# Five raw buffers of streamed fp32 blocks as one tile with strictly rotating slots, in a single-core DiT block

## The chip, the cores and the metric

The kernel runs on one core of one Trainium2 chip. The metric is the device time of one execution in microseconds. A NeuronCore has TensorE (PE, with its weight loads shown apart as PEld), VectorE (DVE), ScalarE (ACT), GpSimd (POOL) and SyncE (SP). SP here does little else than issue DMAs, one after the other, from one instruction queue.

## What is computed

One layer of a diffusion transformer on 256 latent and 256 context tokens, width 2048, all in fp32, followed by a final norm. The reference, cut down:

```python
mod = (silu(c) @ w_ada + b_ada)[:, None, :]
sh1, sc1, g1, sh2, sc2, g2 = split(mod, 6)
h = modulate(rmsnorm(x, norm1_g), sh1, sc1)           # context tokens likewise
dq, dk, dv, mq, mk, mv, ga, gb = project(h, w_in, w_uq, w_ukv)
o_da  = diff_attend(dq, dk_all, dv_all, lam)          # 8 heads, two softmax maps each
o_mla = softmax_attend(mq, mk_all, mv_all, MLA_SCALE) # 8 heads, low-rank q and kv
x = x + g1 * ((sigmoid(ga) * (o_da @ w_o_da) + sigmoid(gb) * (o_mla @ w_o_mla)) @ w_out)
x = x + g2 * ((silu(h2 @ w_gate) * (h2 @ w_up)) @ w_down)
return rmsnorm(x, final_norm_g)
```

Two streams of HBM data matter here: the weights of the big projections, and `w_ada`, of which the kernel needs a matrix-vector product (a gemv) for each modulation vector.

## The kernel before, in words

**Weights.** Every projection is a sum over k of weight blocks of 128 x 1024 fp32 values (512 KB). `load_w` (line 159) takes a buffer tagged `raw` from the pool `stream`, which has five of them, and issues one DMA on SP (line 161). `split_w` (line 164) divides the block into a high part `wh`, cast by ACT (line 169), and a low part `wl`, which DVE gets by subtracting `wh` from `raw` (line 170). TensorE then multiplies three products, wh by the activations' high and low parts and wl by the high part, in `GroupT` and `group_b` (matmuls at lines 155 and 157). `wh` and `wl` have three buffers each. One block, called a unit below, feeds 24 matmuls: 16 with wh and 8 with wl. The last reader of a raw buffer is the subtraction on DVE.

**Gemv blocks.** `gemv` (line 495) streams `w_ada` in blocks of the same shape through the same five `raw` buffers (DMA at line 503) and accumulates on DVE: `gacc = raw * c + gacc` (line 507, and line 505 for the first of 16). One gemv block has one reader only, this DVE operation, whose output every next one needs. The gemv is a Python generator that runs in the background. A stage calls `tick` (line 371), and each tick writes the next block's DMA and accumulation into the program. Through attention and through the gate, output and merge projections (`ga`, `gb`, `yab`, lines 835 to 852, and `wo`, lines 874 to 893), three chunks of `w_ada` are worked off in this way. In the `ga`, `gb` and `yab` stages `every(2)` (line 376) gives one gemv block per two weight units. In the FFN, from the third of eleven column groups on, `gate.rest(tick)` (line 949) gives one gemv block per gate unit, for chunk 5.

**Order.** The Tile scheduler sets the order of the instructions on each engine, not the source alone. It works with the buffers' releases: a tile of the tag `raw` gets the buffer that comes free first, so which buffer a load takes is decided while scheduling. Each load's DMA waits for the DVE operation that last read its buffer, and SP issues the loads in its fixed order.

**The lead.** For a DMA into a raw buffer, count on DVE the operations that read raw blocks (lines 170, 505 and 507) from the one that releases the buffer to the one that reads the new block. That count is called the lead of the load below. A load with lead 3 is issued when the third raw-reading operation before its own reader has ended.

**Attention.** For the four pairs of heads `p` of the differential attention the program puts the projections of the next pair, gemv blocks and the softmax on the same engines. On DVE the splits `dvl` (line 548) and the maximum (line 641) stand in order with wl and gacc. ACT's exponential (line 642) waits for the maximum, and the scores' matmuls (`ps`, line 676) wait for ACT to have read the bank.

Of the kernel before, what the change touches and what calls it, by code (L numbers as in the profile page):

```python
# [11 lines left out]
F32 = mybir.dt.float32  # L12
# [6 lines left out]
P = 128  # L19
# [77 lines left out]
def kernel(  # L97
# [9 lines left out]
    def pool(name, bufs=1, space=None, side=None):  # L107
        st = ExitStack()
        kw = {}
        if space is not None:  # L110
            kw["space"] = space
        if side is not None:
            kw["side"] = side
        pl = st.enter_context(tc.tile_pool(name=name, bufs=bufs, reuse_waits="tile", **kw))
        return pl, st.close
# [3 lines left out]
    stream, _c1 = pool("stream")  # L119
# [19 lines left out]
    def nm(s):  # L139
        uid[0] += 1  # L140
        return f"{s}{uid[0]}"


    class Acc:
# [6 lines left out]
        def mm(self, region, lhsT, rhs, last=False):  # L151
# [4 lines left out]
            else:  # L156
                nc.tensor.matmul(region, lhsT, rhs, start=False, stop=last, skip_group_check=key != self.lead)  # L157

    def load_w(src, a, n):
        raw = stream.tile([P, 1024], F32, tag="raw", name=nm("raw"), bufs=5)  # L160
        nc.sync.dma_start(out=raw[:, : a * n], in_=src)
        return raw[:, : a * n].rearrange("p (a n) -> p a n", a=a)

# [9 lines left out]
    def wunit(w, k0, a, c0, n):  # L173
        return split_w(load_w(w.block(k0, a, c0, n), a, n), a, n)
# [257 lines left out]
    def first_group(k0, nk):  # L432

        v = load_w(w_in.block(k0, nk, 3584, 320), nk, 320)
        wh = stream.tile([P, 1024], F32R, tag="wh", name=nm("wh"), bufs=3)
        wl = stream.tile([P, 1024], F32R, tag="wl", name=nm("wl"), bufs=3)
# [4 lines left out]
        nc.scalar.copy(h1[:, :, 320:], h1[:, :, 256:320].bitcast(F32))  # L441
        nc.scalar.copy(l1[:, :, 320:], l1[:, :, 256:320].bitcast(F32))
        h2, l2 = split_w(load_w(w_in.block(k0, nk, 1024, 512), nk, 512), nk, 512)

        def cut(i, n):
# [49 lines left out]
    def gemv(chunk, sink):  # L495


        for hf in range(2):
            a = const.tile([P, 1024], F32, tag="gacc", name=nm("gacc"), bufs=1)
            c0 = chunk * D + hf * 1024  # L500
            for kt in range(KT):
                raw = stream.tile([P, 1024], F32, tag="raw", name=nm("raw"), bufs=5)
                nc.sync.dma_start(out=raw, in_=w_ada[kt * P : (kt + 1) * P, c0 : c0 + 1024])
                if kt == 0:
                    nc.vector.tensor_scalar_mul(a, raw, cols[:, kt : kt + 1])
                else:
                    nc.vector.scalar_tensor_tensor(a, raw, cols[:, kt : kt + 1], a, op0=ALU.mult, op1=ALU.add)  # L507
                if kt < KT - 1:
                    yield
            yield from sink(hf, a)  # L510
# [158 lines left out]
    def da_attention(h, q, k, v):  # L669
# [23 lines left out]
        split(oTa[0][:, h, :], oTa[1][:, h, :], y)  # L693

    bg[0] = chain(gemv(2, to_cols(g1c, 2)), gemv(4, to_cols(sc2c, 4)), gemv(3, to_cols(sh2c, 3)))
    for p in range(4):
        if p == 0:
# [230 lines left out]
    def keep(hf, a):  # L928
# [7 lines left out]
        yield  # L936

    bg[0] = gemv(5, keep)

    for g in range(11):  # L940
# [96 lines left out]
```

## Time and profile before

| what | us |
|---|---|
| runs of the kernel | 1600.13, 1592.73, 1602.61 |
| their median | 1600.13 |
| the profiled execution | 1590.97 |
| its span, first to last instruction | 1589.2 |

The profile shows the one profiled execution. Times in rows are microseconds from the span's start. A row of the timeline has start, busy time, engine, line, operation, tiles, and in brackets how long the engine was idle before it and what ended that. "x2" in such a row means two operations drawn together. `SPq` and the like are an engine's instruction queue, where DMAs are issued. Matmul ends are modelled, so a busy TensorE says that it had work, not that it ran at its peak.

### The profile page before, as it was taken

The page shows a single profiled execution, that of the slowest core. Times are in us where ns is not written, and L with a number is a line of the kernel's source. Part 1 is how long each engine was busy: PE and PEld are TensorE (multiplying, and loading weights), DVE is VectorE, ACT ScalarE, POOL GpSimd, SP SyncE. Part 2 cuts the span into 40 slices and gives each one's busy share as a digit, 9 for nine tenths or more (in the row PEclk, how much of TensorE's full clock was granted, in tenths as well). Part 3 has the DMA queues.
Part 4 walks back from the last instruction along what each step waited for, and adds up shares of the span by engine and source line. Part 5 has one row for each costly group of instructions (what it writes and reads, how often), then busy time and mean ns, then how long its engine had stood idle before and what let it go on. Part 6 is the DMA issues. An engine that isn't in the chain of part 4 may idle for free.

```text
span 1589.2 us, 28863 instructions
## 1 busy us (share of the span) xinstructions
PE 1536.9 (97%) x11966; PEld 1443.3 (91%) x11966; DVE 1015.8 (64%) x1360; ACT 736.8 (46%) x1038; POOL 16.1 (1%) x14
## 2 busy tenths in 40 slices
PE   3899999998999999999999999999999999999997
PEld 2678899998899999999999999999999999888886
DVE  5437887787896667677777566767555545455454
ACT  4335455545675444444446444444444444344343
POOL 0000000000000000000000000000000000011010
PEclk9999999999999999999999999999999999999999
DMA  9894653456454787878884668888566656665563
GB/s 369 338 366 161 210 176 111 139 176 202 150 160 162 258 280 259 291 266 296 299 280 148 229 226 300 289 271 280 196 191 196 197 192 220 194 192 197 191 193 120
DMA packets 100595, 356.34 MB, mean 224 GB/s; under 512 B 10993, under 2 KB 13553, under 8 KB 100209
## 3 DMA queue, kind: packets, MB, share of 16 engines
q1 hardware_dynamic: 99600, 351.58, 65.9%
q10 hardware_dynamic: 864, 2.93, 0.5%
q8 instruction: 93, 1.52, 0.4%
q14 instruction: 38, 0.30, 0.1%
HBM read 352.37 MB, written 2.10 MB: 223 GB/s over the span
## 4 chain that ended last, share of the span: by engine, by line
PE 72%; DMA 9%; DVE 6%; issue 1%; ACT 1%; DVEq 0%; POOLq 0%; POOL 0%; ACTq 0%
PE gate L157 15%; PE up L157 15%; PE down L157 15%; DMA raw<-in_w_ada_dram 9%; PE ga L157 4%; PE dv L157 4%; PE gb L157 3%; DVE gacc L507 3%; PE dk L157 2%; DVE wl L170 2%; PE yab L157 2%; PE wo L157 2%; PE dq L157 1%; PE cq L157 1%; PE pt L647 1%
## 5 line engine op out<-in xcount | busy, mean ns | idle before, releaser
L170 DVE TENSOR_TENSOR wl<-raw,wh 128x1024 fp32r<-128x1024 f32 (+1 forms) x453 | 548.9, 1222 | 326.9 <-ACT wh L169 312.6
L169 ACT CAST wh<-raw 128x1024 fp32r<-128x1024 f32 (+1 forms) x453 | 474.9, 1051 | 572.7 <-PE down L157 134.9
L507 DVE SCALAR_TENSOR_TENSOR gacc<-raw,cols,gacc 128x1024 f32<-128x1024 f32 x120 | 154.0, 1283 | 123.5 <-DMA raw<-in_w_ada_dram 123.2
L157 PE MATMUL gate<-h,wh 128*128 128x256 f32 x1386 | 175.9, 277 | 0.0
L157 PE MATMUL up<-h,wh 128*128 128x256 f32 x1386 | 175.8, 277 | 0.0
L157 PE MATMUL down<-wh,hid 128*128 128x512 f32 x696 | 173.3, 389 | 0.0
L157 PEld LDWEIGHTS up<-h,wh 128*128 128x128 f32 x1386 | 166.4, 188 | 0.1
L157 PEld LDWEIGHTS gate<-h,wh 128*128 128x128 f32 x1386 | 166.5, 188 | 0.0
L157 PEld LDWEIGHTS down<-wh,hid 128*128 128x128 f32 x696 | 130.7, 188 | 27.0
L157 PE MATMUL gate<-h,wl 128*128 128x256 f32 x704 | 96.7, 277 | 0.0
L157 PE MATMUL up<-h,wl 128*128 128x256 f32 x704 | 96.7, 277 | 0.0
L157 PE MATMUL down<-wl,hid 128*128 128x512 f32 x352 | 94.6, 389 | 0.0
L157 PEld LDWEIGHTS up<-h,wl 128*128 128x128 f32 x704 | 87.8, 188 | 0.2 <-DVE wl L170 0.2
L157 PEld LDWEIGHTS gate<-h,wl 128*128 128x128 f32 x704 | 87.8, 188 | 0.1
L157 PEld LDWEIGHTS down<-wl,hid 128*128 128x128 f32 x352 | 66.1, 188 | 13.7
L157 PE MATMUL ga<-hl,wh 128*128 128x256 f32 x504 | 65.6, 278 | 0.0
L157 PE MATMUL wo<-mT,wh 128*128 128x256 f32 x504 | 64.2, 278 | 0.0
L157 PE MATMUL gb<-hl,wh 128*128 128x256 f32 x504 | 64.0, 278 | 0.0
L157 PEld LDWEIGHTS ga<-hl,wh 128*128 128x128 f32 x504 | 61.4, 188 | 0.6 <-ACT wh L169 0.4
L157 PEld LDWEIGHTS wo<-mT,wh 128*128 128x128 f32 x504 | 60.6, 188 | 0.4 <-issue 0.4
L157 PEld LDWEIGHTS gb<-hl,wh 128*128 128x128 f32 x504 | 60.7, 188 | 0.0
L408 PE MATMUL pgb<-sraw,c 128*32 128x512 f32 (+1 forms) x288 | 32.8, 597 | 17.4 <-DMA sraw<-in_w_mod_dram 17.4
(334 smaller groups left out, 2316.5 us busy)
## 6 DMA issues: line engine op xcount, KB each, us to landing
raw<-in_w_ada_dram SPq DMA_DIRECT2D x128, 512.0 KB, 4.2
raw<-in_w_in_dram SPq DMA_DIRECT2D x119, 512.0 KB, 4.6
raw<-in_w_ffn_gate_dram SPq DMA_DIRECT2D x88, 512.0 KB, 4.4
raw<-in_w_ffn_up_dram SPq DMA_DIRECT2D x88, 512.0 KB, 4.4
raw<-in_w_ffn_down_dram SPq DMA_DIRECT2D x88, 512.0 KB, 3.6
sraw<-in_w_mod_dram SPq DMA_DIRECT2D x64, 512.0 KB, 8.5
raw<-in_w_out_dram SPq DMA_DIRECT2D x32, 512.0 KB, 5.1
raw<-in_w_o_da_dram SPq DMA_DIRECT2D x16, 512.0 KB, 4.8
```

The costliest lines, as they stand in the source:

```text
L157: nc.tensor.matmul(region, lhsT, rhs, start=False, stop=last, skip_group_check=key != self.lead)
L169: nc.scalar.copy(h, v)
L170: nc.vector.tensor_sub(l, v, h.bitcast(F32))
L408: nc.tensor.matmul(pgb[32 * j : 32 * j + 32, :w], c32[:, kt, :], vs[kt], start=kt < 4, stop=kt >= 12, tile_position=(0, 32 * j))
L507: nc.vector.scalar_tensor_tensor(a, raw, cols[:, kt : kt + 1], a, op0=ALU.mult, op1=ALU.add)
L647: nc.tensor.transpose(pt[:, j * P : (j + 1) * P], a[:, j * P : (j + 1) * P], ident)
```

## The change

The five `raw` buffers are no longer five tiles of a pool. They are one tile `raws` of 128 x 5 x 1024 values, allocated once, and a function hands out its five slots strictly in turn, in the order in which the loads are written in the program. Both users, `load_w` and `gemv`, call it. The memory is the same size, the number and shape of DMAs, casts, subtractions, accumulations and matmuls is the same.

```diff
+    raws = stream.tile([P, 5, 1024], F32, name="raws")
+    loads = [0]
+
+    def raw_tile():
+
+        loads[0] += 1
+        return raws[:, loads[0] % 5, :]
+
     def load_w(src, a, n):
-        raw = stream.tile([P, 1024], F32, tag="raw", name=nm("raw"), bufs=5)
+        raw = raw_tile()
         nc.sync.dma_start(out=raw[:, : a * n], in_=src)
...
             for kt in range(KT):
-                raw = stream.tile([P, 1024], F32, tag="raw", name=nm("raw"), bufs=5)
+                raw = raw_tile()
                 nc.sync.dma_start(out=raw, in_=w_ada[kt * P : (kt + 1) * P, c0 : c0 + 1024])
```

All later lines move down by eight: line 161 of before is 169 of after, 170 is 178, 503 is 511, 507 is 515, 548 is 556, 641 is 649. The order of SP's 681 DMAs differs at 228 places, all in the stretches where gemv blocks run beside weights. In the FFN's column groups 6 to 10 and in the down projection the order is the same as before.

The DMA issues on SP in the second of the four `ga`/`gb`/`yab` groups, four gemv blocks (`in_w_ada`) and the eight weight units of `w_o_da` and `w_o_mla` that they alternate with. Before:

```order
241 L503 DMA raw_7009<-in_w_ada_dram 128x1024
242 L161 DMA raw_7017<-in_w_o_da_dram 128x1024
243 L161 DMA raw_7047<-in_w_o_da_dram 128x1024
244 L503 DMA raw_7077<-in_w_ada_dram 128x1024
245 L161 DMA raw_7080<-in_w_o_da_dram 128x1024
246 L161 DMA raw_7110<-in_w_o_da_dram 128x1024
247 L503 DMA raw_7140<-in_w_ada_dram 128x1024
248 L161 DMA raw_7147<-in_w_o_mla_dram 128x1024
249 L161 DMA raw_7177<-in_w_o_mla_dram 128x1024
250 L503 DMA raw_7207<-in_w_ada_dram 128x1024
251 L161 DMA raw_7210<-in_w_o_mla_dram 128x1024
252 L161 DMA raw_7240<-in_w_o_mla_dram 128x1024
```

The same twelve loads after the change:

```order
188 L511 DMA raws<-in_w_ada_dram 128x1024
189 L169 DMA raws<-in_w_o_da_dram 128x1024 x3
190 L511 DMA raws<-in_w_ada_dram 128x1024
191 L169 DMA raws<-in_w_o_da_dram 128x1024
192 L169 DMA raws<-in_w_o_mla_dram 128x1024
193 L511 DMA raws<-in_w_ada_dram 128x1024
194 L169 DMA raws<-in_w_o_mla_dram 128x1024 x2
195 L511 DMA raws<-in_w_ada_dram 128x1024
196 L169 DMA raws<-in_w_o_mla_dram 128x1024
```

Before, a gemv load stands first of its three and takes the slot that its own predecessor's accumulation leaves. After, a weight load stands in that place. The gemv load stands one or two places later and takes the slot that a weight's subtraction leaves.

Counted over both programs, the leads of the 128 gemv loads are:

| lead | 1 | 2 | 3 | 4 | 5 | 6 and more |
|---|---|---|---|---|---|---|
| gemv loads before | 4 | 17 | 64 | 25 | 14 | 4 |
| gemv loads after | 1 | 37 | 33 | 32 | 16 | 9 |

In the first of the four `ga`/`gb`/`yab` groups four gemv loads lose one lead and one gains two, in the second (561 to 632 us of the trace) six lose one and two gain one, in the third four lose one and three gain one. In `wo` one loses and one gains. In each of the four FFN groups with gemv two lose one, and two later ones gain one.

The DVE instructions ahead of the softmax of the fourth pair in attention, from the gemv accumulations to the first maxima (`c<-ps`). Before:

```order
460 L507 SCALAR_TENSOR_TENSOR gacc_3632<-raw_4455,cols,gacc_3632 128x1024
461 L507 SCALAR_TENSOR_TENSOR gacc_3632<-raw_4488,cols,gacc_3632 128x1024
462 L170 TENSOR_TENSOR wl_4395<-raw_4392,wh_4394 128x1024
463 L507 SCALAR_TENSOR_TENSOR gacc_3632<-raw_4521,cols,gacc_3632 128x1024
464 L170 TENSOR_TENSOR wl_4428<-raw_4425,wh_4427 128x1024
465 L548 TENSOR_TENSOR dvl_4170<-dv_3939,dvh_4169 128x256
466 L548 TENSOR_TENSOR dvl_4170<-dv_3940,dvh_4169 128x256
467 L641 TENSOR_REDUCE c_4188<-ps_4184 128x1
```

The same place after the change:

```order
458 L515 SCALAR_TENSOR_TENSOR gacc_3569<-raws,cols,gacc_3569 128x1024 x2
459 L178 TENSOR_TENSOR wl_4312<-raws,wh_4311 128x1024
460 L515 SCALAR_TENSOR_TENSOR gacc_3569<-raws,cols,gacc_3569 128x1024
461 L556 TENSOR_TENSOR dvl_4090<-dv_3867,dvh_4089 128x256
462 L556 TENSOR_TENSOR dvl_4090<-dv_3868,dvh_4089 128x256
463 L649 TENSOR_REDUCE c_4108<-ps_4104 128x1
```

The subtraction `wl` that stood directly ahead of `dvl` (row 464 of before) stands behind the maxima in the changed program.

## Rows read from the trace of the kernel before

**Rows 1.** The page's first lines: span, busy time of each engine, share, instructions.
```profile
span 1589.2 us, 28863 instructions
...
PE 1536.9 (97%) x11966; PEld 1443.3 (91%) x11966; DVE 1015.8 (64%) x1360; ACT 736.8 (46%) x1038; POOL 16.1 (1%) x14
```

**Rows 2.** Busy time by stretch; columns: stretch, length, PE, PEld, DVE, ACT, POOL, clock, DMA share, GB/s.
```profile
0.00:40.00 40.00, 15.65 (x101) 8.89 (x102) 22.04 (x45) 17.09 (x27) 0.73 (x5) 0.91 0.97 369
600.00:640.00 40.00, 38.53 (x335) 37.59 (x334) 29.64 (x29) 15.94 (x17) 0.00 (x0) 1.00 0.81 266
1100.00:1140.00 40.00, 40.00 (x351) 39.82 (x351) 22.31 (x22) 18.07 (x19) 0.00 (x0) 1.00 0.64 209
```

**Rows 3.** The page's costliest groups, DVE; busy, mean ns of one, idle before, releaser.
```profile
L170 DVE TENSOR_TENSOR wl<-raw,wh 128x1024 fp32r<-128x1024 f32 (+1 forms) x453 | 548.9, 1222 | 326.9 <-ACT wh L169 312.6
...
L507 DVE SCALAR_TENSOR_TENSOR gacc<-raw,cols,gacc 128x1024 f32<-128x1024 f32 x120 | 154.0, 1283 | 123.5 <-DMA raw<-in_w_ada_dram 123.2
```

**Rows 4.** Timeline of DVE, second ga/gb/yab group, then third.
```profile
601.20 1.28 DVE L507 SCALAR_TENSOR_TENSOR gacc<-raw,cols,gacc 128x1024 f32<-128x1024 f32 x1 [2.59 <-DMA raw<-in_w_ada_dram]
602.40 2.36 DVE L170 TENSOR_TENSOR wl<-raw,wh 128x1024 fp32r<-128x1024 f32 x2
606.20 1.28 DVE L507 SCALAR_TENSOR_TENSOR gacc<-raw,cols,gacc 128x1024 f32<-128x1024 f32 x1 [1.43 <-DMA raw<-in_w_ada_dram]
...
624.02 1.28 DVE L507 SCALAR_TENSOR_TENSOR gacc<-raw,cols,gacc 128x1024 f32<-128x1024 f32 x1 [2.98 <-DMA raw<-in_w_ada_dram]
...
716.93 2.35 DVE L170 TENSOR_TENSOR wl<-raw,wh 128x1024 fp32r<-128x1024 f32 x2
```

**Rows 5.** Timeline of SP's DMA issues in the same group.
```profile
602.51 0.33 SPq L503 DMA_DIRECT2D raw<-in_w_ada_dram  x1
603.65 1.47 SPq L161 DMA_DIRECT2D raw<-in_w_o_mla_dram  x2
```

**Rows 6.** Timeline of PE, first matmuls with a wl, second and third group.
```profile
628.90 1.21 PE L157 MATMUL ga<-hl,wl 128*128 128x256 f32 x8 [1.36 <-DVE wl L170]
...
696.20 1.20 PE L157 MATMUL ga<-hl,wl 128*128 128x256 f32 x8 [0.37 <-DVE wl L170]
...
718.20 1.20 PE L157 MATMUL gb<-hl,wl 128*128 128x256 f32 x8
```

**Rows 7.** The gemv loads at line 503: time from issue to landing.
```profile
DMA to landing us min/median/max: 3.3/4.2/6.4
```

**Rows 8.** Timeline of DVE, end of the FFN's gate groups 2 to 5.
```profile
961.42 2.38 DVE L170 TENSOR_TENSOR wl<-raw,wh 128x1024 fp32r<-128x1024 f32 x2
...
1004.85 1.22 DVE L170 TENSOR_TENSOR wl<-raw,wh 128x1024 fp32r<-128x1024 f32 x1
...
1049.52 2.41 DVE L170 TENSOR_TENSOR wl<-raw,wh 128x1024 fp32r<-128x1024 f32 x2
...
1095.66 1.22 DVE L170 TENSOR_TENSOR wl<-raw,wh 128x1024 fp32r<-128x1024 f32 x1
```

**Rows 9.** Timeline of PE, the matmuls that use those wl.
```profile
963.35 0.62 PE L157 MATMUL gate<-h,wl 128*128 128x256 f32 x4
...
1006.87 0.62 PE L157 MATMUL gate<-h,wl 128*128 128x256 f32 x4
...
1052.94 0.64 PE L157 MATMUL gate<-h,wl 128*128 128x256 f32 x4
...
1098.16 0.64 PE L157 MATMUL gate<-h,wl 128*128 128x256 f32 x4
```

**Rows 10.** Timeline of DVE ahead of the fourth pair's softmax.
```profile
368.55 1.28 DVE L507 SCALAR_TENSOR_TENSOR gacc<-raw,cols,gacc 128x1024 f32<-128x1024 f32 x1 [2.43 <-DMA raw<-in_w_ada_dram]
369.75 1.22 DVE L170 TENSOR_TENSOR wl<-raw,wh 128x1024 fp32r<-128x1024 f32 x1
370.89 0.75 DVE L548 TENSOR_TENSOR dvl<-dv,dvh 128x256 fp32r<-128x256 f32 x2
```

**Rows 11.** Timeline of PE at that softmax.
```profile
373.10 0.80 PE L676 MATMUL ps<-dk,dq 128*128 128x512 f32 x1 [5.96 <-ACT t L642]
```

## The prediction

> **What bounds the kernel now.** I read the page first. TensorE is busy 1536.9 of 1589.2 us, 97%, and DVE 64% [rows 1], so the kernel is bound by TensorE nearly everywhere. The table of stretches says where it is not. In the first 40 us TensorE works 15.65 us, with the DMA engines at 0.97: that is the start, where weights come in, and the change doesn't reorder it. From 600 to 640 us it works 38.53 of 40, and in the FFN without gemv 40.00 of 40 [rows 2]. The reader is to see from this that there is little to win. TensorE is idle for 1589.2 - 1536.9 = 52.3 us [rows 1], of which 40 - 15.65 = 24.4 lie in the first 40 us [rows 2]. The other 28 us, 1.8%, are all there is, and the largest gap among them that the change touches is the 5.96 us of [rows 11]. What the change can do more easily is to lengthen waits.
>
> The costliest DVE groups say which waits there are. The accumulation gacc costs 1283 ns and was idle for 123.5 us in 120 runs, nearly all for its own block's DMA. The subtraction wl costs 1222 ns [rows 3]. DVE works in order, so while gacc waits for a gemv block the wl behind it waits too, and wl is what TensorE needs. In the second ga/gb/yab group a round of one gemv block and two weight units goes like this: gacc starts at 601.20 after a wait of 2.59 us, the two wl take 2.36, the next gacc waits 1.43 and starts at 606.20 [rows 4]. SP issues the gemv load at 602.51, when gacc at 601.20 has ended, and the two weight loads at 603.65 and after [rows 5]. So the gemv load goes out as soon as its predecessor is accumulated and uses the two wl as cover (lead 3). TensorE at first doesn't feel it, since wl run ahead of it. But such rounds take a little longer than TensorE's two units, the advance is used up, and at 628.90 TensorE waits 1.36 us for wl, in the next group 0.37 at 696.20 [rows 6]. At 718.20 [rows 6] it uses a wl that ended at about 718.15, the first of the two in the row at 716.93 [rows 4]. DVE sets the pace at these points, and what comes on top of its rounds there is paid in full.
>
> **What the change does to this, part by part.** The instructions are the same in number and shape, so nothing is added or removed on any engine, and the slots are the same 512 KB. What changes is the slot that a load takes. Before, a load takes the first free buffer. A gemv load gets the one that its own predecessor leaves, as gaccs run ahead of the wl of weights written earlier in the program. After, it takes the slot of the load five before it in the written order, which mostly is a weight's. That slot is free one DVE operation later. The order pieces show it: weight loads move ahead, the gemv load one or two places back.
>
> *The price of one lost lead.* The load is issued 603.65 - 602.51 = 1.14 us later [rows 5], by one wl. Whether the wait of gacc grows by 1.14 depends on how long the load takes. The trace shows 3.3 us at least, 4.2 in the median and 6.4 at most [rows 7]. If the later load, with fewer loads behind it, took 3.3 where it took 4.2, the price is 1.14 - 0.9 = 0.2 us. If it took 6.4, because a weight load is now in flight ahead of it, it is 1.14 + 2.2 = 3.3 us. I take 1.2, near the 1.14 of the issue with an unchanged median, as the gemv load has one weight load about 1.1 us from it in either order: before it stood behind, now it stands ahead. A gained lead gives back the same, if gacc waited there.
>
> *Second group.* Six gemv loads lose a lead. Two gain one: the first at 624.02, where gacc waited 2.98 us [rows 4] and gives 1.2 back, the second behind the point that counts. At 628.90 TensorE already waits, so the sum is paid there: (6 - 1) x 1.2 = 6.0 us.
>
> *Third group.* Two losses and a gain stand ahead of 696.20, where TensorE waits 0.37 us: 1.2 us. Behind it a gain and two losses come before 718.20, where wl is just in time: 1.2 us. Together 2.4. The last gain of this group lies where nothing waits. The first group loses four and gains two, but the timeline of TensorE shows no gap there that ends on a wl, so I take nothing. In wo one loss and one gain cancel.
>
> *FFN groups with gemv.* Each has two losses and, for certain, one gain: 1.2 us against the advance at the gate's end. With 1.22 us for one wl [rows 3], the wl of the gates' last units end at 962.64, 1006.07, 1050.74 and 1096.88 [rows 8], and TensorE uses them at 963.35, 1006.87, 1052.94 and 1098.16 [rows 9]: advances of 0.7, 0.8, 2.2 and 1.3. That makes 0.5 + 0.4 = 0.9 us, and groups 4 and 5 cover it.
>
> *Attention.* Ahead of the fourth pair's softmax, gacc at 368.55 waited 2.43 us, the wl at 369.75 follows, and dvl, with the maxima among it, starts at 370.89 [rows 10]. ACT's exponential follows the maximum, and TensorE stands 5.96 us for it [rows 11]. After the change one wl (370.89 - 369.75 = 1.14 us) stands behind the maximum and not ahead of it: -1.1 us. The last gacc there has lead 1 now, but its release is a wl that ends where the load of before was issued, so its landing stays where it was. In the rest of attention more gemv loads gain a lead than lose one, and I take nothing.
>
> *Sum.* 6.0 + 2.4 + 0.9 - 1.1 = +8.2 us. The profiled execution took 1590.97 us, which becomes 1599.2. That execution lies 9.2 us below the median of the runs, 1600.13, as does the shortest run, 1592.73; the runs of this kernel spread over 10 us. I put the sum on the median: 1608.3 us. It is +0.5%. A measurement can tell about 1% here, 16 us.
>
> On a load's own time: the Trainium skill, DMA: Bandwidth & Descriptors, section "Anatomy of one DMA", gives a fixed 2.0 us plus the bytes at 436 GB/s for a DMA alone, which as an estimate is 3.2 us for 512 KB. The shortest gemv load of this trace, 3.3 us, agrees. By that figure a load that gets the DMA engines to itself costs 1.14 - 1.0 = 0.1 us for a lost lead, and the sum would be near zero.
>
> **The rivals.**
>
> *No net change.* The loads get shorter as much as they are issued later, price about 0.2. Then the same sum is 5 x 0.2 + 2 x 0.2 - 1.1 = +0.3 us, 1600 us. For it: DMA share is 0.81 there [rows 2] and a load's time runs from 3.3 to 6.4, so it depends on what is in flight. Against it: the weight load that was behind the gemv load is now ahead of it, and shares the engines with it while it is under way.
>
> *Slower, over the 1%: SP's queue and shared DMA engines.* Place: the in-order issue on SP in the second and third group. A weight load that stands ahead of the gemv load on SP holds it, when its own slot is late, and takes bandwidth from it. The price is then up to 3.3 us a round. With more than 2.2 us a price the FFN groups all pay: 4 times the price less their advances of 0.7 + 0.8 + 2.2 + 1.3 = 5.0. Together 5p + 2p + 4p - 5.0 - 1.1, at 3.3 that is +30 us, 1630 us. It passes 16 us at p = 2.0. For it: 228 of SP's 681 DMAs change place, in many places a weight load moves one or two rows ahead. Against it: those weight loads wait for slots that gacc left, which are free early.
>
> A rule of the Trainium skill bears on this rival: the same page and section says that DMA engines don't wait on semaphores, the wait stands on the issuing sequencer. By that rule a late slot of one weight load holds each DMA behind it on SP. No row here shows SP's wait with its price.
>
> *Faster.* The attention gap closes (5.96 us [rows 11]) and the waits at 628.90 and 696.20 go (1.36 + 0.37 [rows 6]), because the gained leads hit the right places: 1600.1 - 7.7 = 1592 us. For it: lead 2 rises, but lead 4 too, and the gap's maxima move ahead of a wl. Against it: in the groups losses are more than gains, and they stand ahead of the waits. It wouldn't reach 1% even then.
>
> *The change doesn't do what it says.* If the slots of one tile were released only together, every load would wait for all five readers, and the streams would stall by far more. The built order shows SP's loads interleaved with the same kind of wait for one DVE operation, so I give this nothing of its own and leave it inside the slower case.
>
> **How the numbers follow.** Forecast (+8, price around 1.2): 0.50. No net change: 0.20. Slower over 1%: 0.20. Faster: 0.10. The first two and nearly all of the faster case lie within 1%. From the forecast's own upper side, a price of 2.0 or more, I give 0.02 to slower. Faster over 1% needs 16 of the 28 us that TensorE idles behind the start, twice what the faster case names, so 0.02. That leaves slower 0.22 and within 1% 0.76. The range leaves a tenth on either side. Below, it goes to 1593, the faster case. Above, it goes to 1627, a price of about 3.0. The forecast's own range, at prices from 0.6 to 1.8, is 1603 to 1614 us.
>
> **What would show it right or wrong.** Right: in the second group gacc waits about 1.2 us longer in the rounds whose load lost a lead, SP's gemv issue comes one wl after the predecessor's end, and TensorE's wait at the third unit of the next ga grows from 1.36 to some 7 us, perhaps split over several units. The gap ahead of the fourth softmax shrinks from 5.96 to about 5. The FFN without gemv and the down projection stay as they are. Wrong: gacc's waits sum to 123 us as before (then landing times took it up), or TensorE's idle time grows where the order is unchanged, or gemv loads take over 5 us to land in most rounds (then the slower rival).

## The result, and the profile after

| | before | after |
|---|---|---|
| runs, us | 1600.13, 1592.73, 1602.61, 1596.93 | 1614.87, 1612.21, 1624.30, 1611.69 |
| median, us | 1598.53 | 1613.54 |
| profiled execution, us (span) | 1590.97 (1589.2) | 1614.87 (1613.1) |

The changed kernel is slower: the ratio is 1.0146, 95% interval 1.0114 to 1.0177. The ratio is the one on record and not the quotient of the two medians, which differ by 15.0 us, 0.9%; on 1598.5 us it would be some 23 us. The time of 1613.5 us lies in the range of the prediction, and the sign is the one that it gave. The size is not: +8.2 us were forecast, and the two profiled executions differ by 23.9 us.

Where the time went is read from the first matmuls of each stage. The table has the distance between them in the two profiles, in us, with differences taken before rounding. Two of its borders are others: the stretch with gemv in the FFN ends at the last matmul on the gemv's own output (tile `gs`), just ahead of group 5's up units, and the down projection at its last matmul.

| stretch | before | after | difference |
|---|---|---|---|
| start, modulation, attention, up to the first gb unit | 508.6 | 510.7 | +2.1 |
| ga/gb/yab groups, up to the first wo unit | 247.0 | 261.1 | +14.1 |
| wo, up to the first gate unit | 99.7 | 99.9 | +0.3 |
| FFN groups 0 and 1, no gemv | 88.1 | 88.1 | 0.0 |
| FFN groups 2 to 5, to the gemv's last matmul | 157.4 | 164.7 | +7.3 |
| rest of the FFN, no gemv | 239.6 | 239.6 | 0.0 |
| down projection | 239.2 | 239.2 | 0.0 |

So 21.4 of 23.9 us lie where gemv blocks run beside weights and TensorE is the bound, and nothing in the parts of the FFN and the down projection that have no gemv. The 2.1 us ahead of the groups come from the start, before the first gemv load (see below).

The page after, first its engines, then the DVE groups and the gemv loads that answer to [rows 1], [rows 3] and [rows 7]:

```profile
span 1613.1 us, 28853 instructions
PE 1547.2 (96%) x11966; PEld 1449.4 (90%) x11966; DVE 1015.1 (63%) x1360; ACT 733.6 (45%) x1038; POOL 16.1 (1%) x14
...
L178 DVE TENSOR_TENSOR wl<-raws,wh 128x1024 fp32r<-128x1024 f32 (+1 forms) x453 | 548.3, 1221 | 325.9 <-ACT wh L177 309.6
...
L515 DVE SCALAR_TENSOR_TENSOR gacc<-raws,cols,gacc 128x1024 f32<-128x1024 f32 x120 | 153.9, 1282 | 148.9 <-DMA raws<-in_w_ada_dram 148.6
...
DMA to landing us min/median/max: 3.3/4.7/6.6
```

The operations take what they took. gacc waits 148.6 us for its blocks where it waited 123.2, and a gemv load lands 4.7 us after its issue in the median where it took 4.2.

The timeline of DVE in the second group after the change, which answers to [rows 4]:

```profile
596.72 1.28 DVE L515 SCALAR_TENSOR_TENSOR gacc<-raws,cols,gacc 128x1024 f32<-128x1024 f32 x1 [0.54 <-DMA raws<-in_w_ada_dram]
597.93 2.35 DVE L178 TENSOR_TENSOR wl<-raws,wh 128x1024 fp32r<-128x1024 f32 x2
604.05 1.28 DVE L515 SCALAR_TENSOR_TENSOR gacc<-raws,cols,gacc 128x1024 f32<-128x1024 f32 x1 [3.77 <-DMA raws<-in_w_ada_dram]
605.25 2.35 DVE L178 TENSOR_TENSOR wl<-raws,wh 128x1024 fp32r<-128x1024 f32 x2
611.89 1.28 DVE L515 SCALAR_TENSOR_TENSOR gacc<-raws,cols,gacc 128x1024 f32<-128x1024 f32 x1 [4.29 <-DMA raws<-in_w_ada_dram]
```

and SP's DMA issues there, which answer to [rows 5]:

```profile
596.22 2.15 SPq L169 DMA_DIRECT2D raws<-in_w_o_da_dram  x2
599.17 0.33 SPq L511 DMA_DIRECT2D raws<-in_w_ada_dram  x1
600.31 0.33 SPq L169 DMA_DIRECT2D raws<-in_w_o_da_dram  x1
605.36 0.33 SPq L169 DMA_DIRECT2D raws<-in_w_o_mla_dram  x1
606.50 0.33 SPq L511 DMA_DIRECT2D raws<-in_w_ada_dram  x1
```

The two views belong together. gacc starts at 604.05 and ends at 605.33. At 605.36 SP issues a weight load, as the slot that gacc left is the weight's now. At 606.50, when the first wl behind gacc has ended, it issues the gemv load. This lands 5.30 us later, and the next gacc has waited 4.29 us when it starts at 611.89. SP holds nothing back here: each of these issues stands right behind the end of a DVE operation that reads a raw slot.

TensorE in the second group and the third, which answer to [rows 6]:

```profile
581.14 1.20 PE L157 MATMUL gb<-hl,wl 128*128 128x256 f32 x8 [0.41 <-DVE wl L178]
...
588.88 1.18 PE L157 MATMUL gb<-hl,wl 128*128 128x256 f32 x8 [2.02 <-DVE wl L178]
589.90 2.39 PE L157 MATMUL gb<-hl,wh 128*128 128x256 f32 x12
...
632.44 1.20 PE L157 MATMUL ga<-hl,wl 128*128 128x256 f32 x8 [1.17 <-DVE wl L178]
...
727.13 2.08 PE L157 MATMUL gb<-hl,wl 128*128 128x256 f32 x8 [2.25 <-DVE wl L178]
```

It waits for wl ten times in the groups, 10.8 us in all (gaps of over 0.15 us), where before it waited twice, 1.7 us. Each of the ten wl stands on DVE directly behind an accumulation that had waited 1.85 to 4.88 us for its own block. For the wait at 588.88 these are the rows:

```profile
586.40 1.29 DVE L515 SCALAR_TENSOR_TENSOR gacc<-raws,cols,gacc 128x1024 f32<-128x1024 f32 x1 [4.18 <-DMA raws<-in_w_ada_dram]
587.61 3.49 DVE L178 TENSOR_TENSOR wl<-raws,wh 128x1024 fp32r<-128x1024 f32 x3
```

ACT's casts waited longer for weight DMAs too, 132 us over the whole kernel where it was 53, but these ten wl start without a gap behind gacc, so a late cast is not what held them.

Behind the wait at 588.88, twelve matmuls take 2.39 us. This is the granted clock, in the table of stretches of the changed kernel (columns as in [rows 2]):

```profile
588.00:590.00 2.00, 1.12 (x9) 1.12 (x10) 2.00 (x3) 1.79 (x2) 0.00 (x0) 1.00 0.61 184
590.00:594.00 4.00, 4.00 (x23) 4.00 (x22) 1.33 (x2) 0.00 (x0) 0.00 (x0) 0.57 0.87 279
```

From 590 to 594 us the mean is 0.57, most of it at the lower level of 1.2 GHz. Of the 23 matmuls counted there 21 start in it. At one start every 0.113 us, as in the FFN without gemv (last section), it would be 35. That wait cost 2.0 us as a gap and (35 - 21) x 0.113 = 1.6 us behind it. The wait at 727.13 is followed by the same: granted clock 0.50 from 728 to 730. Behind the gaps of 1.84 us (614.37) and 1.69 us (690.64) it stays at 1.00.

### The profile page after: what moved, and what is told of

Same layout as the page of the kernel before. It is cut to its first block, busy times and chain, and to the rows that moved or that the text cites. A ratio compares the mean times of both kernels' runs of the same rounds, so it can differ in the third digit from the quotient of the medians.

```text
span 1613.1 us, 28853 instructions
## 1 busy us (share of the span) xinstructions
PE 1547.2 (96%) x11966; PEld 1449.4 (90%) x11966; DVE 1015.1 (63%) x1360; ACT 733.6 (45%) x1038; POOL 16.1 (1%) x14
## 4 chain that ended last, share of the span: by engine, by line
PE 70%; DMA 9%; DVE 6%; issue 3%; ACT 1%; DVEq 0%; POOLq 0%; POOL 0%; ACTq 0%; SPq 0%
PE down L157 14%; PE up L157 14%; PE gate L157 11%; DMA raws<-in_w_ada_dram 7%; PE ga L157 4%; PE wo L157 4%; DVE wl L178 4%; PE gb L157 4%; PE dv L157 3%; PE dk L157 3%; PE yab L157 2%; PE dq L157 1%; DVE gacc L515 1%; DMA raws<-in_w_o_mla_dram 1%; PE cq L157 1%
## 5 line engine op out<-in xcount | busy, mean ns | idle before, releaser
L178 DVE TENSOR_TENSOR wl<-raws,wh 128x1024 fp32r<-128x1024 f32 (+1 forms) x453 | 548.3, 1221 | 325.9 <-ACT wh L177 309.6
L177 ACT CAST wh<-raws 128x1024 fp32r<-128x1024 f32 (+1 forms) x453 | 473.7, 1050 | 614.4 <-PE down L157 134.7
L515 DVE SCALAR_TENSOR_TENSOR gacc<-raws,cols,gacc 128x1024 f32<-128x1024 f32 x120 | 153.9, 1282 | 148.9 <-DMA raws<-in_w_ada_dram 148.6
```

The costliest lines, as they stand in the source:

```text
L177: nc.scalar.copy(h, v)
L178: nc.vector.tensor_sub(l, v, h.bitcast(F32))
```

## The experiments

All of them are the changed kernel's single tile with other slots, unless the text says more. A slot is given by a list, one digit a load:

```diff
-        loads[0] += 1
-        return raws[:, loads[0] % 5, :]
+    slots = ("...134120134120134120...")
+        loads[0] += 1
+        return raws[:, int(slots[loads[0] - 1]), :]
```

The digits shown are a piece of those that the pool of before gave in the ga/gb/yab groups, where the loads are written as weight, weight, gemv. The gemv block has slot 1 each time here, and the weights use 3, 4, 2 and 0 in turn. Through most of the groups the pool had given the gemv a slot of its own without anybody asking for it. With five slots strictly in turn and a period of three, the load five before a gemv load is a weight's, always.

**The tile alone.** The list of before, for all 598 loads. SP's loads and DVE's operations then stand in the order of before at every place.

> The changed kernel's single tile, but its five slots handed out by a list: the slots that the pool of the kernel before gave, load by load. Theory (the turn costs time, because a gemv load takes a weight's slot): the time of before, 1598 us within 8, gacc's idle time near 123 us and TensorE's waits for wl at two places of the ga/gb/yab groups. Rival (the one tile itself costs, by its dependencies or addresses): the time of the changed kernel, about 1613 us, with gacc's idle time near 149 us.

Measured: ratio 0.9991 (0.9959 to 1.0024), median 1591.2 us of ten runs against 1592.2. The groups took 244.8 us, the FFN with gemv 157.4. gacc's row on this kernel's page:

```profile
L522 DVE SCALAR_TENSOR_TENSOR gacc<-raws,cols,gacc 128x1024 f32<-128x1024 f32 x120 | 153.9, 1282 | 116.5 <-DMA raws<-in_w_ada_dram 116.1
```

So one tile in place of five costs nothing. The order of the slots is all of it.

**The turn in the groups and wo only.** The list is strict turn from the first ga unit to the end of wo, before's pattern elsewhere.

> Strict turn only from the first ga unit to the end of wo, the slots of before elsewhere. Theory (a lost lead costs some 2.4 us of gacc's wait, and the second and third ga/gb/yab groups pay it in full): 13 to 15 us above the slots of before, some 1612 us, the FFN as before. Rival (the price is 1.2 us, as forecast, and the rest is noise between executions): +8 us, 1606. Rival (the groups only look late because of the stages ahead): no more than +3 us.

Measured: ratio 1.0096 (1.0061 to 1.0130). The groups took 259.5 us, 12.5 more than before, wo 103.8, the FFN with gemv 156.9. The theory's +13 to +15 us is met (0.0096 x 1592 = 15.3), the two rivals' +8 and +3 lie below the interval (9.7 to 20.7). Of the 12.5 us in the groups 2.2 are the slower rate of matmuls told of in the last section, and none is a lower granted clock.

**The turn in the FFN only.**

> Strict turn only from the first FFN load on, the slots of before elsewhere. Theory: the four FFN groups with gemv pay some 1 to 2.5 us each, +6 to +7 us, some 1605 us; the six groups without gemv and the down projection take the time of before. Forecast's price of 1.2 us: +1 us. Rival (slots in turn slow the plain weight stream too): more than +10 us, with the difference still growing after the last gemv block.

Measured: ratio 1.0022 (0.9996 to 1.0048), which alone can't be told from none. The profile can: the FFN groups with gemv took 164.7 us, to a tenth what they take in the changed kernel, and every other stretch of the FFN is as before (88.1, 239.6, 239.2). The ratios of this run and the last add to 1.012, just inside the interval of the full change.

**Weights three slots, gemv two.**

The gemv has slots 3 and 4 in turn, the weights 0, 1 and 2. A piece of the list, from the groups:

```diff
+    slots = ("...312401320412301420...")
```

> Five slots of one tile, split by use: weights take three in turn, gemv blocks two in turn. Every gemv load then takes a slot that an earlier gemv block left (leads mostly 3, 4 and 5 or more, two of them 2). Theory (the gemv's lead decides): gacc's idle time falls well below 123 us, to 20 to 70 us, and TensorE's waits for wl in the groups go, unless the weights with three slots come late; 1592 to 1600 us. Rival (a load five back is late for whichever stream, so fewer weight slots cost as much): ACT's cast waits for weight DMAs and the time is 1610 us or more.

Measured: ratio 1.0064 (1.0032 to 1.0095), median 1601.9. gacc's wait fell as expected:

```profile
L522 DVE SCALAR_TENSOR_TENSOR gacc<-raws,cols,gacc 128x1024 f32<-128x1024 f32 x120 | 153.8, 1281 | 55.8 <-DMA raws<-in_w_ada_dram 53.9
```

But the time did not: it lies above the theory's 1592 to 1600 and below the rival's 1610. Of 123 us of gacc's waits before, TensorE felt no more than its few gaps on wl, and taking the waits away buys little. FFN groups 0 and 1, where only weights are loaded, took 94.7 us against 88.1: 3.5 us are waits at the first gate units, one of them for a late cast, and some 2.8 the slower rate of matmuls told of below. The rival has a part in it: casts waited 164 us for weight DMAs, where before it was 53.

**Weights four slots, gemv one, everywhere.**

> One tile of five slots by a simple rule: gemv blocks always take the fifth, weights take the other four in turn. Theory (a gemv load should take the slot that a gemv block left; in the ga/gb/yab groups the pool of before did just that): there the leads are 3 again, those groups take some 247 us as before and not 261, the FFN groups with gemv near 157 us; in all 1592 to 1600 us. Rival (weights in turn over fewer slots lose as much as the gemv wins): 1605 us or more, with casts that wait for weight DMAs.

Measured: ratio 1.0016 (0.9988 to 1.0044). The groups took 248.3 us and TensorE has no gap of over 0.15 us in them. Of these 248.3 us some 4 more than before are the slower rate of matmuls. gacc's waits came to 151.5 us over the kernel, as many as in the changed kernel, but 56.8 of them lie in the groups (before 54.6, changed kernel 77.5) and 51.0 in the FFN (before 25.3), where the stretch with gemv has one gap of TensorE on a wl, 1.72 us: it is not their sum that counts, but whether wl have an advance where they stand. In the groups the 45 lead-3 loads waited 1.74 us each, as before. The FFN groups 0 and 1 took 92.8, 4.4 of it waits (for h at their begin, for wl in their second half). Attention was the surprise: 499.6 us to the first gb unit against 508.6.

**Half a gemv load.** The strict turn, with 512 of 1024 columns loaded. The kernel leaves out half of `w_ada`.

```diff
-                nc.sync.dma_start(out=raw, in_=w_ada[kt * P : (kt + 1) * P, c0 : c0 + 1024])
+                nc.sync.dma_start(out=raw[:, :512], in_=w_ada[kt * P : (kt + 1) * P, c0 : c0 + 512])
```

> The changed kernel with gemv loads of 512 of the 1024 columns; the second half of the vector products is made from what lies in the slot, so the modulation vectors are not those of the reference. DVE's operations keep their size. The scheduler gives more gemv loads lead 2 (58 against 37). Theory (the price of a lost lead is 1.1 us of later issue and the rest a longer landing, as a weight load goes out 1.1 us ahead and shares the DMA engines): a half load lands in some 3.5 us instead of 4.7, gacc's wait in lead-2 rounds falls from about 3.8 to about 2.6 us, the groups take less than 261 us in spite of more lead-2 loads, 253 or so. Rival (the wait comes from SP's queue, which holds the gemv load behind a weight load): the waits stay near 3.8 us and the groups take 261 us or more.

Measured: ratio 1.0227 (1.0173 to 1.0281), groups 265.4 us. On the time the expectation was wrong. The scheduler had put 36 lead-2 loads into the groups and wo, where the changed kernel has 14, and I had set their number too low against the shorter wait. On the wait it was right: in rounds with lead 2 gacc waited 2.72 us (mean of 36) against 3.79 (mean of 14), and the loads landed in 3.95 us against 5.01. The wait falls by what the landing falls, 1.07 and 1.06 us. With a wait that came from SP's queue it would not have.

**Two more slots for the gemv in the groups.** The slots of before, but between the first ga unit and the last yab unit the gemv takes two slots of a further tile and the weights take all five.

```diff
+    gemvp, close_gemv = pool("gemvp")
+    more.append(gemvp.tile([P, 2, 1024], F32, name="more"))
     yp, close_yp = pool("yp")
```

> The slots of before, but in the ga/gb/yab groups the gemv blocks have two slots of their own in a further tile and the weights take all five in turn. Theory (gacc's wait is what lengthens the rounds there, and TensorE sets the pace without it): gacc hardly waits in the groups, TensorE doesn't wait for wl there, the groups take 243 to 246 us against 247 of before and 261 of the changed kernel; the whole 1 to 4 us under before, which a measurement can't tell from none. Rival (more loads in flight slow each other and the casts wait): groups of 248 us or more.

Measured: ratio 1.0010 (0.9977 to 1.0043), groups 248.3 us, which is the rival's number. TensorE waited for wl only once there, 0.31 us. What lengthened the groups in this execution was the matmuls' rate (below): 1112 intervals at the slower rate against 387 before, some 3.2 us. Without them the groups are some 2 us shorter than before. gacc's waits in the groups came to 28.0 us where it was 54.6, not to nearly none as expected, and TensorE hardly felt those that were left. So nothing more was to be had: the groups of before were already at TensorE's own pace but for some 2 us.

**The old slots where they are good, an own slot where that is better.** Up to the end of wo gemv one slot and weights four in turn, then the list of before.

> One tile of five slots: up to the end of wo gemv blocks have a slot of their own and weights take the other four in turn, from the FFN on the slots of before. The run with this rule throughout took 499.6 us to the first gb unit against 508.6 before, as TensorE's gap of 5.96 us ahead of the fourth pair's softmax was gone, and lost 5 us at the FFN's begin and 1 us in its gemv groups, where four weight slots are few. Theory (both are due to the slots): 8 to 11 us less than before, a ratio of 0.993 to 0.996. Rival (the gap of attention closes by chance of one execution): 1.000.

Measured: ratio 0.9980 (0.9951 to 1.0009), above the expected 0.993 to 0.996 and not told from the rival's 1.000. Attention was 499.5 us again, wo 104.9. The same, with the slots of before from wo on:

> As the run before, but the slots of before begin at wo already. Theory: the same 8 to 11 us less than before (0.993 to 0.996), wo 99 to 100 us instead of 102. Rival: 1.000.

Measured: ratio 0.9969 (0.9943 to 0.9995), median 1589.6 us of twelve runs against 1593.2. That is just below before, by less than expected, and 1.7% below the changed kernel by the two ratios. Attention took 499.4 us, wo 104.1 and not 99 to 100, which gave back 4 of the 9 us: TensorE's gaps there came to 4.4 us where it was 2.0, and behind the one of 2.41 us the granted clock fell to the 1.2 GHz level for 3 to 4 us. DVE ahead of the fourth pair's softmax in this kernel, against [rows 10]:

```profile
355.86 1.29 DVE L522 SCALAR_TENSOR_TENSOR gacc<-raws,cols,gacc 128x1024 f32<-128x1024 f32 x1 [3.73 <-DMA raws<-in_w_ada_dram]
...
360.73 1.28 DVE L522 SCALAR_TENSOR_TENSOR gacc<-raws,cols,gacc 128x1024 f32<-128x1024 f32 x1 [2.45 <-DMA raws<-in_w_ada_dram]
361.93 1.22 DVE L185 TENSOR_TENSOR wl<-raws,wh 128x1024 fp32r<-128x1024 f32 x1
363.07 0.75 DVE L563 TENSOR_TENSOR dvl<-dv,dvh 128x256 fp32r<-128x256 f32 x2
```

dvl starts at 363.07 where it started at 370.89, and TensorE's gap of 5.96 us [rows 11] isn't there. Two accumulations that wait stand ahead of dvl from 352 us on, where before there were three (at 361.01, 363.70 and 368.55). The waits themselves are no shorter, 3.73 and 2.45 us, so it is one accumulation fewer ahead of the softmax that goes with the closed gap. The three kernels with one slot of the gemv's own there all took 499.4 to 499.6 us, so it is no accident of one execution.

## Why the prediction was right in sign and wrong in size

**The mechanism held.** A gemv load takes a weight's slot, its issue stands one wl later, gacc waits longer, wl are late, and TensorE waits. The runs with the tile alone (no cost), the turn in the groups (+12.5 us there) and the turn in the FFN (+7.3 us there) show place and cause, and the rows ahead of TensorE's waits show the path. Of the signs that the prediction named these came true: the gemv load goes out one wl behind its predecessor's end, gacc waits longer in such rounds, and the FFN without gemv and the down projection stay as they are. The start's +2.1 us are of another kind: the changed kernel's profile falls behind by that much between 56 and 60 us, at a granted clock of 0.50, ahead of the first gemv load at 143.8, and the run with the turn in the FFN shows it too, whose loads there have the slots of before.

**The price of a lost lead was the step that failed.** It was put at 1.2 us: 1.14 of later issue and an unchanged landing. The waits, grouped by the lead of the load (the lead from the built order, wait and landing from the timelines, 500 to 850 us; loads with more lead had no wait), are:

| lead | before: loads, mean wait, mean landing | after: loads, mean wait, mean landing |
|---|---|---|
| 2 | 1, 2.92, 4.99 | 14, 3.79, 5.01 |
| 3 | 42, 1.74, 4.29 | 26, 1.36, 4.90 |
| 4 | 6, 0.19, 4.18 | 11, 0.19, 4.86 |

From lead 3 of before to lead 2 of after the wait grows by 2.05 us. 0.72 of it is the landing (5.01 - 4.29). The other 1.33 is cover that is gone, of which the later issue, by one wl, is 1.14. The forecast had argued that the gemv load has a weight load 1.1 us from it in either order, so that the landing wouldn't change. It changes. Gemv loads with one raw load still on its way when they were issued (500 to 1120 us, 24 before and 30 after) landed in 3.7 us in the median before and in 4.8 after. What differs is the age of that other load: after, in 20 of the 30 it had been issued less than 1.5 us earlier, and these gemv loads landed in 5.1 us, the other 10 in 3.7. Before it was so in 3 of 24; the other 21 landed in 3.6. A load that follows another by some 1.1 us lands later than one that goes ahead. This is the part of the slower rival that was true, shared DMA engines. Its other part, SP holding the gemv load, is not in the issues above. The Trainium skill (DMA: Bandwidth & Descriptors, "Anatomy of one DMA") puts a DMA's semaphore wait on the issuing sequencer; the trace agrees, as each gemv issue from 500 to 850 us stands under 0.1 us behind the end of a DVE operation that reads a raw slot, but here this queue was never the late one. The fit that the prediction took from that section of the Trainium skill, 3.2 us for a load alone, is given there for DMAs issued by GpSimd; these are issued on SP. The price near 0.1 that it drew from the figure needed the later load to be alone, and it was not.

In sum over the groups and wo gacc waited 42 x 1.74 + 2.92 + 6 x 0.19 = 77 us before and 14 x 3.79 + 26 x 1.36 + 11 x 0.19 = 91 after. That this is near what TensorE lost there, 14.1 + 0.3, means little: in the groups alone the waits grew by 22.9 us, in wo they fell by 7.7. The forecast had 6.0 + 2.4 = 8.4. By the delay of one profile against the other, the second group came out near its 6.0: from +2.5 us ahead of it to +9.1 at the wl that TensorE uses at 628.90 before. The piece from there to the wl used at 718.20 brought 7.1 us where 2.4 stood. Some 1.6 us of each is the clock. In the run with the turn in the groups, where the clock didn't fall, the same two pieces brought 6.1 and 6.3. So the price alone doesn't give the places. At 2.05 us the forecast's five net losses would be 10.3 us in the second group and its two in the third 4.1. The sum is about right and the split is not: how much of a loss an advance covers was mis-set as well.

**The FFN term failed in its place too.** Forecast +0.9, measured +7.3. The price there was 2.77 - 1.10 = 1.67 us (12 loads each, lead 2 after and lead 3 before). The forecast set two losses less a gain against the advance of wl at the gate's last unit. The losses stand at its second and third accumulation, ahead of the gain. The advance itself was no smaller there than what the forecast took: before, wl of the third gate unit of groups 2 to 5 ended 1.1, 1.4, 3.0 and 1.6 us ahead of their use, against 0.7, 0.8, 2.2 and 1.3 at the last. After, TensorE has eight gaps of over 0.15 us in this stretch, 5.0 us in all, where before it had none. Four are waits for wl of the third and seventh gate units of groups 3 and 5, 2.1 us. One is for a late cast ahead of group 2's up units, 1.2 us. Three are at the matmuls on the gemv's own output, 1.7 us. DVE's order moved as well. The changed kernel's rows in group 2:

```profile
955.73 1.28 DVE L515 SCALAR_TENSOR_TENSOR gacc<-raws,cols,gacc 128x1024 f32<-128x1024 f32 x1 [2.38 <-DMA raws<-in_w_ada_dram]
956.93 2.35 DVE L178 TENSOR_TENSOR wl<-raws,wh 128x1024 fp32r<-128x1024 f32 x2
...
963.34 1.29 DVE L515 SCALAR_TENSOR_TENSOR gacc<-raws,cols,gacc 128x1024 f32<-128x1024 f32 x1 [3.46 <-DMA raws<-in_w_ada_dram]
...
965.75 2.35 DVE L178 TENSOR_TENSOR wl<-raws,wh 128x1024 fp32r<-128x1024 f32 x2
```

and those of before:

```profile
938.32 1.28 DVE L507 SCALAR_TENSOR_TENSOR gacc<-raw,cols,gacc 128x1024 f32<-128x1024 f32 x1 [1.48 <-DMA raw<-in_w_ada_dram]
939.53 1.22 DVE L170 TENSOR_TENSOR wl<-raw,wh 128x1024 fp32r<-128x1024 f32 x1
941.11 1.29 DVE L507 SCALAR_TENSOR_TENSOR gacc<-raw,cols,gacc 128x1024 f32<-128x1024 f32 x1 [0.36 <-DMA raw<-in_w_ada_dram]
942.31 1.22 DVE L170 TENSOR_TENSOR wl<-raw,wh 128x1024 fp32r<-128x1024 f32 x1
```

Before, wl and gacc alternate here and these two gacc wait 1.48 and 0.36 us. After, two wl stand together behind two long waits. The gain of the later loads comes when TensorE has already waited, in group 5:

```profile
1106.82 1.19 PE L157 MATMUL gate<-h,wl 128*128 128x256 f32 x8 [1.10 <-DVE wl L178]
```

**A wait can cost more than its length.** The forecast priced a wait of TensorE at its gap. Behind both gaps of over 2 us in the groups the granted clock fell to the 1.2 GHz level for 3 to 4 us, worth some 1.6 us each time. No such term was in the sum, although the gap of attention was in the rows. It is not a fixed price: of the twelve gaps of 2.0 to 3.1 us that the profiles of the changed kernel and of the runs above show between 500 and 1500 us, eight came with a fall and four did not, one of 3.13 us among them (wo of the first run of the own slot up to there). And the run with the turn in the groups lost 12.5 us there without it.

**Attention came out by luck.** TensorE's gap at the fourth pair's softmax went from 5.96 to 4.99 us, close to the -1.1 us of the forecast. But four of the runs above have the order of before up to there, and their gaps are 4.24 (the tile alone), 5.73 and 5.64 (the turn in the groups, in the FFN) and 6.08 (two more slots), so one order alone gives more than that difference. The run with the tile alone:

```profile
373.70 0.80 PE L691 MATMUL ps<-dk,dq 128*128 128x512 f32 x1 [4.24 <-ACT t L657]
```

The reason given doesn't hold either. After the change:

```profile
355.31 2.60 DVE L515 SCALAR_TENSOR_TENSOR gacc<-raws,cols,gacc 128x1024 f32<-128x1024 f32 x2
...
370.96 1.28 DVE L515 SCALAR_TENSOR_TENSOR gacc<-raws,cols,gacc 128x1024 f32<-128x1024 f32 x1 [4.21 <-DMA raws<-in_w_ada_dram]
372.16 0.75 DVE L556 TENSOR_TENSOR dvl<-dv,dvh 128x256 fp32r<-128x256 f32 x2
...
374.37 0.79 PE L684 MATMUL ps<-dk,dq 128*128 128x512 f32 x1 [4.99 <-ACT t L650]
```

and the accumulations of before that answer to the first row:

```profile
354.57 2.60 DVE L507 SCALAR_TENSOR_TENSOR gacc<-raw,cols,gacc 128x1024 f32<-128x1024 f32 x2
```

From there to dvl it took 16.85 us after and 370.89 - 354.57 = 16.32 before, with one wl fewer. The forecast had the last accumulation's landing stay where it was, but its wait grew from 2.43 [rows 10] to 4.21 us, and the wl that moved was paid back in longer waits. dvl is about 1.1 us sooner only against a profile that runs 2.4 us behind since the start, and that was gained ahead of 355 us, where the forecast took nothing. Attention as a whole gained 0.2 us (+2.1 us at its end, 2.3 of them from the start).

**The rivals.** No net change and faster are out. The slower one, given 0.20 with a price of up to 3.3 and a limit of 2.0, had the better price, 2.05 in the groups, for half of its reason. Whether its 1% was passed depends on the measure: by the ratio yes, by the medians just not.

What stays open: how the groups' loss splits between the second and the third, and how much of the FFN's 7.3 us is the order of wl on DVE and how much the wait. The runs don't separate them, and an order of DVE that is fixed by hand was not tried.

## What to carry to other kernels

A buffer rotation is a statement on who waits for whom. When two streams with different readers share one rotation, count for each load which reader frees its slot and how many operations of the waiting engine lie between: with five slots and a pattern of period three it was always the other stream's. In these groups the stream whose reader delays the critical engine was better off with a slot that its own predecessor frees (247 and 248 us against 261). That was no rule for the whole kernel: one slot for the gemv everywhere left the weights four and gained nothing (1.0016). Extra slots were of no use where TensorE was the bound (1.0010). Price a lost lead by the later issue plus the longer landing behind whatever now goes first. Set each loss against the advance where it falls, and count a gain only from where it stands. Before you take a gap that shrank as proof, see how far it moves between runs with the same order.

## What was not expected of the hardware

TensorE's matmuls run at one of two rates though the granted clock is shown as 1.00 both times. Two executions of the same FFN stretch, without gemv, in the kernel before and in the run with the turn in the groups only (same instructions there), columns as in [rows 2]:

```profile
1140.00:1180.00 40.00, 40.00 (x356) 40.00 (x355) 20.20 (x19) 17.75 (x19) 0.00 (x0) 1.00 0.59 193
```

```profile
1140.00:1180.00 40.00, 40.00 (x342) 40.00 (x341) 19.65 (x19) 17.35 (x19) 0.00 (x0) 1.00 0.58 187
```

356 matmuls in 40 us against 342, 4% fewer: one starts every 113 ns or every 118. All 239.6 us of the FFN behind the gemv became 249.0 in the latter, as they did in two other runs (weights four and gemv one; the own slot up to the end of wo). Which stretches have it differs between executions. It comes to some 10 us, as much as the runs of one kernel spread, and what sets it isn't shown by any run. A stage's length holds it too: of the matmul starts in the groups 387 stand at the slower rate before, 334 after the change and 882 in the run with the turn in the groups. Stage lengths and gaps in the profiles are the safer measure for effects of this size once these intervals are counted out.
